# The down projection of a feed-forward layer as a 2x2 block product with seven products

## The chip, the core and the metric

One core of a Trainium2 chip runs the kernel. The metric is the time of one execution on the device in microseconds (us), the median of three runs. Four engines matter here: TensorE (PE in the rows, with its weight loads as PEld), VectorE (DVE), ScalarE (ACT) and GpSimd (POOL). SyncE (SP) issues nearly all transfers; its queue is SPq in the rows.

## What is computed

Two layers follow each other; the change touches the end of the second one, its feed-forward part:

```
h = rmsnorm(x, norm2_g)                                    # x: 512 tokens x 2048
x = x + (silu(h @ ffn_w_gate) * (h @ ffn_w_up)) @ ffn_w_down   # 2048 -> 5632 -> 2048
return rmsnorm(x, final_norm_g)
```

The down projection is the last product: 512 x 5632 by 5632 x 2048. All of it is float32. The kernel gets float32 precision out of TensorE by writing each operand as a high part h and a residual l in a rounded format (`split`, L136 and L122: ScalarE copies to h, VectorE subtracts h from the raw value to get l) and by adding up three products: high by high, high by residual, residual by high. So every block product costs three matmuls.

## The kernel before

Each matmul multiplies a 128x128 stationary tile by a 128x512 moving tile. A program-wide planner orders the instructions of each engine's queue by priority and by its own idea of durations, and puts in all waits; an engine's queue then runs strictly in that order. `high_priority(n)` moves the instructions under it n places ahead.

The feed-forward part runs in `finish` in two stages.

*Gate and up.* The 5632 hidden features are done in 11 groups of 512. `fast_group` treats gate and up weights of a group together, as a 2x2 block product in which eight block products are replaced by seven, each of a sum of operands by a sum of weights. Operand sums are made once (`fast_operands`, VectorE, then split). Weight sums are made for each group by VectorE (`chained`, L122, the rows fr<-fr,fr), in the raw tiles that the loads filled; the pool of raw tiles has 10 buffers of [128, 2, 512]. `part` then splits a half product's weights (two 128-row tiles, 512 columns) and issues 12 matmuls: eight that use the high weights (pp<-wh), four that use the residual (pp<-wl). I call such a set of 12 a unit. High and residual weights have three buffers each. A product is accumulated in a PSUM tile pp of two banks; there are three such tiles. The finished hidden features are transposed and stored to a scratch tensor in memory, ud.

*Down.* For this stage the raw pool is replaced by one with 3 buffers and PSUM is split anew into eight single banks, tiles psm. A running sum acc (facc in the rows, 512 tokens x 2048) is loaded with the residual stream x3d (L1780). The hidden features come back in 11 chunks of 512 (`hidden`, L1786, two chunks ahead) and are split. For chunks 0 to 9, `down` goes over four blocks of 512 output columns; for each, `block` loads and splits the weights (L146, 512 KB a load) and issues 4 feature tiles x 4 token tiles x 3 = 48 matmuls; VectorE adds the four banks onto acc. Chunk 10 keeps all its weights at hand (L1812) and goes token tile by token tile, so that each tile's final norm and store (L1835) can follow its last add.

All transfers above are issued by SP, in one queue. GpSimd does only small powers for the norms there.

Of the kernel before, what the change touches and what calls it, by code (L numbers as in the profile page):

```python
# [17 lines left out]
D = 2048  # L18
# [75 lines left out]
class Kernel:  # L94
# [1494 lines left out]
    def fast_operands(self, pool, za, zb, tiles):  # L1589
        ta, tb = slice(0, 256), slice(256, 512)  # L1590
        x5 = self.t(pool, [128, 4, 256], F32, "fx5")
        x6 = self.t(pool, [128, 4, 256], F32, "fx6")
        x7 = self.t(pool, [128, 4, 256], F32, "fx7")
# [4 lines left out]
        for i, x in ((1, za[:, :, ta]), (7, x7), (5, x5), (6, x6), (4, None), (3, zb[:, :, tb]), (2, zb[:, :, ta])):  # L1598
            if i == 4:
                x = x7  # L1600
                self.tt(x, zb[:, :, ta], x6, ALU.add)
            o = tiles()
            h, l = (o[:, k:k + 2, :].rearrange("p a (b t) -> p (a b) t", t=256) for k in (0, 2))
            self.split(h, l, x)
            out[i] = (h, l)
        return out


    def halves(self, raw, pools):
        pools.append(pools.pop(0))  # L1610
        h = self.t(pools[0], [128, 2, 512], F32R, "wh")
        l = self.t(pools[0], [128, 2, 512], F32R, "wl")
        self.split(h, l, raw)
        return h, l

    def fast_group(self, srcs, X, rp, cp, wps, parts):
        nc, tc = self.nc, self.tc
        W = {}  # L1620
# [18 lines left out]
        ps = {}  # L1639

        def part(i, u, opens):
            with tc.high_priority(self.ahead):
                h, l = self.halves(weight[i](u), wps)
            at = [(2 * u + kk, kk, t) for kk in range(2) for t in range(2)]

            for j, kk, t in at:
                xh, xl = (x[:, j % 4, t * 128:t * 128 + 128] for x in X[j // 4][i])
                self.mm(ps[i][:, t, :], xh, h[:, kk, :], opens and j == 0, False, not opens)
                self.mm(ps[i][:, t, :], xl, h[:, kk, :], False, False, not opens)
            for j, kk, t in at:  # L1650
                xh = X[j // 4][i][0][:, j % 4, t * 128:t * 128 + 128]
                self.mm(ps[i][:, t, :], xh, l[:, kk, :], False, j == 7, not opens)
# [7 lines left out]
        for p in parts:  # L1660
            for i in (1, 7, 5):
# [4 lines left out]
                if p[-1] == 3 and i == 1:  # L1666
                    p1 = result("p1")
# [28 lines left out]
    def finish(self):  # L1696
        tc, nc, a = self.tc, self.nc, self.a
        NC = 11
# [3 lines left out]
        with self.pool("ff0", 1) as f0:  # L1702
# [3 lines left out]
            with self.pool("opx", 2) as opx:  # L1706
                X = []
                made = [0]

# [4 lines left out]
                with self.pool("w21", 1) as p1, self.pool("w22", 2) as p2, self.pool("w23", 3) as p3:  # L1714
# [3 lines left out]
                    for n, b in enumerate((0, 2, 1, 3)):  # L1718
# [20 lines left out]
                        if n % 2 == 0:  # L1739
                            za = z  # L1740
                        else:
                            X.append(self.fast_operands(p1, za, z, tiles))
# [10 lines left out]
                with self.pool("fr", 10, side="right") as rp, self.pool("fc", 1) as cp, self.pool("fu", 2) as up, self.pool("fw", 1) as fw:  # L1753
# [20 lines left out]
            self.raw_pool = self.pool("wq", 3, side="right")  # L1774
            self.wp = self.raw_pool.__enter__()
            self.psum_pools(4, 4)
            with self.pool("ff1", 2) as p1, self.pool("ff2", 1) as p2:
                acc = self.t(p2, [128, 4, D], F32, "facc")
                for t in range(4):
                    nc.sync.dma_start(out=acc[:, t, :], in_=x3d[t])  # L1780
                fg = self.t(p2, [128, D], F32, "fg")
                nc.sync.dma_start(out=fg, in_=a["final_norm_g_2"].rearrange("(o d) -> o d", o=1).to_broadcast([128, D]))

                def hidden(c):
                    u = self.four(F32)
                    nc.sync.dma_start(out=u, in_=ud[c * 4:c * 4 + 4].rearrange("f p t -> p f t"))  # L1786
                    h4, l4 = self.four(F32R), self.four(F32R)
                    self.split(h4, l4, u)
                    return [(h4[:, j, :], l4[:, j, :]) for j in range(4)]

                def down(c, hs):
                    for b in range(4):
                        ps = [self.psm() for _ in range(4)]
                        self.block(wd[c * 512:c * 512 + 512], [(b * 512, 512)], 4,
                                   [(ps[t], "t", (t, 0), hs, True, True) for t in range(4)])
                        for t in range(4):
                            v = acc[:, t, b * 512:b * 512 + 512]
                            self.tt(v, v, ps[t], ALU.add)

                hs = [hidden(0), hidden(1)]  # L1800
                for c in range(NC - 1):
                    down(c, hs[c])
                    if c + 2 < NC:
                        hs.append(hidden(c + 2))

                c = NC - 1
                W = []
                for b in range(4):
                    h4, l4 = self.four(F32R), self.four(F32R)
                    for k in range(0, 4, 2):  # L1810
                        raw = self.t(self.wp, [128, 2, 512], F32, "raw")
                        nc.sync.dma_start(out=raw, in_=wd[c * 512 + k * 128:c * 512 + k * 128 + 256, b * 512:b * 512 + 512].rearrange("(k p) c -> p k c", p=128))  # L1812
                        self.split(h4[:, k:k + 2, :], l4[:, k:k + 2, :], raw)
                    W.append((h4, l4))
                for t in range(4):
                    s4 = self.t(p1, [128, 4], F32, "s4")
                    tk = slice(t * 128, t * 128 + 128)
                    for b in range(4):
                        ps = self.psm()
                        for k in range(4):  # L1820
                            xh, xl = hs[c][k]
                            self.mm(ps, xh[:, tk], W[b][0][:, k, :], k == 0, False)
                            self.mm(ps, xh[:, tk], W[b][1][:, k, :], False, False)
                            self.mm(ps, xl[:, tk], W[b][0][:, k, :], False, k == 3)
                        v = acc[:, t, b * 512:b * 512 + 512]
                        self.tt(v, v, ps, ALU.add)
                        j = self.t(p1, [128, 512], F32, "g")
                        self.act(j, v, AF.Square, accum_out=s4[:, b:b + 1])
# [3 lines left out]
                    for b in range(4):  # L1832
                        o = slice(b * 512, b * 512 + 512)
                        self.stt(acc[:, t, o], acc[:, t, o], r4, fg[:, o], ALU.mult, ALU.mult)
                        nc.sync.dma_start(out=self.out[0, tk, o], in_=acc[:, t, o])  # L1835
# [33 lines left out]
```

## Time and profile before

| | before |
|---|---|
| median of 3 runs | 3597.96 us (3597.35 to 3599.32) |
| time of the profiled execution | 3597.96 us |
| span of its trace, first to last instruction | 3596.1 us |
| PE busy | 3507.5 us (98%) |
| DVE busy | 2173.8 us (60%) |
| ACT busy | 1368.8 us (38%) |
| mean granted clock of TensorE | 0.985 of full speed |

The profile is of one execution. Busy time of PE is modelled from pipelined matmuls, so a busy PE need not be at its peak. Where the rows name a buffer, the number behind it is left out: wh and wl are high and residual weights, fr and raw are raw weight tiles, op are operand tiles, acc, pp and psm are PSUM tiles.

### The profile page before, as it was taken

The page shows a single profiled execution, that of the slowest core. Times are in us where ns is not written, and L with a number is a line of the kernel's source. Part 1 is how long each engine was busy: PE and PEld are TensorE (multiplying, and loading weights), DVE is VectorE, ACT ScalarE, POOL GpSimd, SP SyncE. Part 2 cuts the span into 40 slices and gives each one's busy share as a digit, 9 for nine tenths or more (in the row PEclk, how much of TensorE's full clock was granted, in tenths as well). Part 3 has the DMA queues.
Part 4 walks back from the last instruction along what each step waited for, and adds up shares of the span by engine and source line. Part 5 has one row for each costly group of instructions (what it writes and reads, how often), then busy time and mean ns, then how long its engine had stood idle before and what let it go on. Part 6 is the DMA issues. An engine that isn't in the chain of part 4 may idle for free.

```text
span 3596.1 us, 48583 instructions
## 1 busy us (share of the span) xinstructions
PE 3507.5 (98%) x18850; PEld 2748.8 (76%) x18850; DVE 2173.8 (60%) x3432; ACT 1368.8 (38%) x2225; POOL 55.7 (2%) x50
## 2 busy tenths in 40 slices
PE   6899999999999999999999998999999999999998
PEld 3486668777778788788877786888888888788887
DVE  3364555456554545675466557777788788555445
ACT  3333443356533323443233334444444444322212
POOL 0000000000000000000000000000000000000000
PEclk8999999999999999999999999999999999999999
DMA  8813333322144353334444443334443344534333
GB/s 278 283 36 112 99 100 88 95 67 82 48 138 147 107 149 109 112 116 116 132 121 129 145 141 129 117 117 127 131 122 107 118 123 141 187 122 126 99 100 106
DMA packets 352602, 442.22 MB, mean 123 GB/s; under 512 B 45871, under 2 KB 200179, under 8 KB 351731
## 3 DMA queue, kind: packets, MB, share of 16 engines
q1 hardware_dynamic: 349456, 437.82, 39.9%
q8 instruction: 148, 2.42, 0.3%
q10 hardware_dynamic: 2915, 1.29, 0.1%
q14 instruction: 83, 0.68, 0.1%
HBM read 383.45 MB, written 55.57 MB: 122 GB/s over the span
## 4 chain that ended last, share of the span: by engine, by line
PE 93%; DMA 3%; DVE 2%; ACT 1%; issue 0%; SPq 0%; POOL 0%; DVEq 0%; ACTq 0%; POOLq 0%
PE acc L112 44%; PE psm L112 23%; PE pp L112 23%; PE psm L116 2%; DMA wm<-in_w_mod_dram 1%; PE pt L116 1%; DVE wl L122 0%; DMA xr<-in_x_dram 0%; DMA raw<-in_ffn_w_down_dram 0%; DMA ym<-ysd 0%; DVE op L122 0%; PE acc L116 0%; DMA xr<-in_ctx_dram 0%; DMA fr<-in_ffn_w_up_dram 0%; DVE s L122 0%
## 5 line engine op out<-in xcount | busy, mean ns | idle before, releaser
L112 PE MATMUL acc<-op,wh 128*128 128x512 f32 (+2 forms) x4160 | 1254.5, 390 | 14.8 <-DVE sl L132 4.6
L112 PEld LDWEIGHTS acc<-op,wh 128*128 128x128 f32 (+1 forms) x4160 | 764.1, 189 | 229.5 <-issue 54.9
L122 DVE TENSOR_TENSOR wl<-raw,wh 128x512 fp32r<-128x512 f32 (+4 forms) x464 | 421.0, 908 | 690.0 <-ACT wh L136 641.1
L112 PE MATMUL acc<-op,wl 128*128 128x512 f32 (+2 forms) x2080 | 773.0, 389 | 2.1 <-DVE wl L122 2.1
L136 ACT CAST wh<-raw 128x512 fp32r<-128x512 f32 (+4 forms) x464 | 369.1, 796 | 1028.3 <-PE acc L112 637.7
L112 PE MATMUL pp<-wh,op 128*128 128x512 f32 x2112 | 529.9, 393 | 10.2 <-ACT wh L136 10.1
L136 ACT CAST wh<-fr 128x1024 fp32r<-128x1024 f32 x308 | 323.1, 1052 | 402.0 <-PE pp L112 350.2
L112 PEld LDWEIGHTS acc<-op,wl 128*128 128x128 f32 (+1 forms) x2080 | 390.4, 189 | 108.7 <-issue 26.9
L112 PEld LDWEIGHTS pp<-wh,op 128*128 128x128 f32 x2112 | 397.4, 188 | 99.3 <-ACT wh L136 10.7
L122 DVE TENSOR_TENSOR wl<-fr,wh 128x1024 fp32r<-128x1024 f32 x308 | 371.1, 1220 | 100.5 <-ACT wh L136 65.5
L112 PE MATMUL psm<-wh,op 128*128 128x512 f32 x1280 | 396.2, 391 | 7.3 <-DVE facc L122 7.3
L112 PEld LDWEIGHTS psm<-wh,op 128*128 128x128 f32 x1280 | 241.4, 189 | 58.2 <-issue 7.7
L112 PE MATMUL pp<-wl,op 128*128 128x512 f32 x1056 | 285.3, 392 | 0.2 <-DVE wl L122 0.2
L112 PE MATMUL psm<-wl,op 128*128 128x512 f32 x640 | 250.1, 391 | 0.3 <-DVE wl L122 0.3
L122 DVE TENSOR_TENSOR fr<-fr,fr 128x1024 f32<-128x1024 f32 x176 | 211.1, 1220 | 50.9 <-DMA fr<-in_ffn_w_gate_dram 33.0
L112 PEld LDWEIGHTS pp<-wl,op 128*128 128x128 f32 x1056 | 197.9, 188 | 43.6 <-DVE wl L122 0.6
L122 DVE TENSOR_TENSOR facc<-facc,psm 128x512 f32<-128x512 f32 x176 | 118.0, 686 | 60.6 <-PE psm L112 54.2
L112 PEld LDWEIGHTS psm<-wl,op 128*128 128x128 f32 x640 | 120.7, 189 | 25.7 <-DVE wl L122 0.7
L112 PE MATMUL acc<-wm,cs 128*32 128x512 f32 x384 | 126.1, 616 | 11.8 <-DMA wm<-in_w_mod_dram 11.8
L112 PE MATMUL acc<-wh,op 128*128 128x256 f32 x576 | 114.8, 293 | 0.0
L112 PEld LDWEIGHTS acc<-wh,op 128*128 128x128 f32 x576 | 91.9, 192 | 5.2 <-issue 3.8
L112 PE MATMUL pp<-wh,opx 128*128 128x512 f32 x352 | 93.8, 399 | 0.0
(469 smaller groups left out, 3506.0 us busy)
## 6 DMA issues: line engine op xcount, KB each, us to landing
raw<-in_w_in_dram SPq DMA_DIRECT2D x216, 256.0 KB, 2.8
fr<-in_ffn_w_gate_dram SPq DMA_DIRECT2D x88, 512.0 KB, 4.1
fr<-in_ffn_w_up_dram SPq DMA_DIRECT2D x88, 512.0 KB, 4.0
raw<-in_ffn_w_down_dram SPq DMA_DIRECT2D x88, 512.0 KB, 3.8
wm<-in_w_mod_dram SPq DMA_DIRECT2D x64, 512.0 KB, 5.8
raw<-in_w_out_dram SPq DMA_DIRECT2D x64, 512.0 KB, 3.8
raw<-in_w_in_dram SPq DMA_DIRECT2D x240, 128.0 KB, 2.4
wm<-in_w_mod_dram SPq DMA_DIRECT2D x64, 256.0 KB, 2.8
```

The lines of the kernel that those rows point to most:

```text
L112: self.nc.tensor.matmul(out, lhsT=l, rhs=r, start=start, stop=stop, skip_group_check=more)
L116: self.nc.tensor.transpose(out, x, self.ident[0:n, 0:n])
L122: (e or self.nc.vector).tensor_tensor(out=out, in0=x, in1=y, op=op)
L136: self.nc.scalar.copy(h, x)
```

## The change

Chunks 0 to 9 of the down stage become five chunks of eight feature tiles (1024 features), each done twice, for the left and the right 1024 output columns (`v`). One such pass is a 2x2 block product (two halves of features, two halves of columns; the 512 tokens are cut into two halves as well) done with seven products in place of eight, in the order 1, 7, 2, 5, 4, 6, 3. Chunk 10 stays as it was, except for its buffers.

Operand sums are made by `fast_operands`, as in the stage before; its temporaries now come from the raw pool. Weight sums are made by transfers: a load puts one block's weights into a raw tile, and a second transfer, issued by GpSimd (`nc.gpsimd.dma_start(..., accum_op=ALU.add)`), adds another block's weights onto them where they lie. Products 7, 6 and 3 reuse the raw tiles of product 1 in that way, each after the split of the product before it in that chain has read them; product 5 adds onto a tile of its own. PSUM and raw pool of the stage before are kept (three tiles of two banks, ten raw tiles), product 2 is accumulated in the bank of product 1, 4 in that of 7, 3 in that of 5. acc is no longer loaded first: in the first chunk the products are copied to it, and then GpSimd's accumulating transfers add x3d.

The twelve matmuls of a unit move into a helper `product`, which the stage before uses too.

```diff
-    def fast_operands(self, pool, za, zb, tiles):
+    def fast_operands(self, temps, za, zb, tiles, order=(1, 7, 5, 6, 4, 3, 2)):
...
-        x5 = self.t(pool, [128, 4, 256], F32, "fx5")
+        x5, x6, x7 = temps(), temps(), temps()
...
+    def product(self, X, i, ps, h, l, j0, opens, last):
+        at = [(j0 + kk, kk, t) for kk in range(2) for t in range(2)]
+
+        for j, kk, t in at:
+            xh, xl = (x[:, j % 4, t * 128:t * 128 + 128] for x in X[j // 4][i])
+            self.mm(ps[:, t, :], xh, h[:, kk, :], opens and j == 0, False, not opens)
+            self.mm(ps[:, t, :], xl, h[:, kk, :], False, False, not opens)
+        for j, kk, t in at:
+            xh = X[j // 4][i][0][:, j % 4, t * 128:t * 128 + 128]
+            self.mm(ps[:, t, :], xh, l[:, kk, :], False, j == last, not opens)
...
-            self.raw_pool = self.pool("wq", 3, side="right")
-            self.wp = self.raw_pool.__enter__()
-            self.psum_pools(4, 4)
             with self.pool("ff1", 2) as p1, self.pool("ff2", 1) as p2:
+                wps = [self.wp2, self.wp2, p2]
                 acc = self.t(p2, [128, 4, D], F32, "facc")
-                for t in range(4):
-                    nc.sync.dma_start(out=acc[:, t, :], in_=x3d[t])
...
+                au = [self.t(p2, [128, 2, 512], F32, f"au{v}") for v in range(2)]
...
+                order = (1, 7, 2, 5, 4, 6, 3)
+
+                def operands(c):
+                    with tc.high_priority(400):
+                        z = []
+                        for i in range(2):
+                            z.append(self.four(F32))
+                            f = (2 * c + i) * 4
+                            nc.sync.dma_start(out=z[i], in_=ud[f:f + 4].rearrange("f p t -> p f t"))
+                        return [self.fast_operands(lambda: raw().rearrange("p a (b t) -> p (a b) t", t=256), z[0], z[1],
+                                                   lambda: self.four(F32R), order)]
+
+                def down(c, v, X):
...
+                    def load(name, u):
+                        r = raw()
+                        nc.sync.dma_start(out=r, in_=source(name, u))
+                        if name == "a11":
+                            W[u] = r
+                        return r
...
+                    def plus(r, name, u):
+                        nc.gpsimd.dma_start(out=r, in_=source(name, u), accum_op=ALU.add)
+                        return r
+
+                    weight = {
+                        1: lambda u: load("a11", u), 7: lambda u: plus(W[u], "a21", u), 2: lambda u: load("a12", u),
+                        5: lambda u: plus(load("a21", u), "a22", u), 4: lambda u: load("a22", u),
+                        6: lambda u: plus(W[u], "a22", u), 3: lambda u: plus(W[u], "a12", u),
+                    }
...
+                    onto = {2: 1, 4: 7, 3: 5}
+                    to = {1: U, 7: A22, 2: A11, 5: A22, 4: A21, 6: U, 3: A12}
+                    for i in order:
+                        ps[i] = ps[onto[i]] if i in onto else bank()
+                        for u in range(2):
+                            with tc.high_priority(self.ahead):
+                                h, l = self.halves(weight[i](u), wps)
+                            self.product(X, i, ps[i], h, l, 2 * u, i not in onto, 3)
+                        if c == 0 and i not in (5, 6):
+                            nc.scalar.copy(to[i], ps[i])
+                        else:
+                            self.tt(to[i], to[i], ps[i], ALU.subtract if i == 5 else ALU.add)
+                    if c == 0:
+                        for t in range(4):
+                            o = slice(v * 1024, v * 1024 + 1024)
+                            nc.gpsimd.dma_start(out=acc[:, t, o], in_=x3d[t][:, o], accum_op=ALU.add)
+                    if c == NC // 2 - 1:
+                        self.tt(A21, A21, U, ALU.subtract)
+                        self.tt(A22, A22, U, ALU.subtract)
+                        self.tt(A12, A12, U, ALU.add)
+
+                X = operands(0)
+                for c in range(NC // 2):
+                    down(c, 0, X)
+                    down(c, 1, X)
+                    if c + 1 < NC // 2:
+                        X = operands(c + 1)
...
                 c = NC - 1
+                with tc.high_priority(400):
...
```

## Rows read from the trace of the kernel before

**Rows 1.** Page, part one: busy time, share and instructions of each engine.

```profile
PE 3507.5 (98%) x18850; PEld 2748.8 (76%) x18850; DVE 2173.8 (60%) x3432; ACT 1368.8 (38%) x2225; POOL 55.7 (2%) x50
```

**Rows 2.** Page, part four: the chain that ended last, by engine.

```profile
PE 93%; DMA 3%; DVE 2%; ACT 1%; issue 0%; SPq 0%; POOL 0%; DVEq 0%; ACTq 0%; POOLq 0%
```

**Rows 3.** Chain in order of time: start, duration (us), what.

```profile
2378.80 16.73 PE pp L112 x73
2396.41 59.48 PE pp L112 x259
...
2457.70 16.79 PE pp L112 x73
...
3125.24 391.31 PE psm L112 x1725
```

**Rows 4.** Waits of TensorE from 2200 us on: total, times, longest.

```profile
PE psm L112 <- DVE facc L122: 10.8, 2, 7.3
```

**Rows 5.** Stretches: PE, PEld, DVE, ACT, POOL, clock, DMA share, GB/s.

```profile
2400.00:2800.00 400.00, 400.00 (x1785) 327.70 (x1784) 319.70 (x293) 180.49 (x193) 0.00 (x0) 1.00 0.40 121
3160.00:3500.00 340.00, 340.00 (x1501) 281.53 (x1501) 169.32 (x191) 72.62 (x66) 0.00 (x0) 1.00 0.36 110
```

**Rows 6.** SP's queue in order of time: two loads of hidden features.

```profile
3190.16 0.37 SPq L1786 DMA_DIRECT2D op<-ud  x1
...
3233.68 0.37 SPq L1786 DMA_DIRECT2D op<-ud  x1
```

**Rows 7.** Groups of instructions from 2200 us on: busy, mean ns, idle before.

```profile
L122 DVE TENSOR_TENSOR fr<-fr,fr 128x1024 f32<-128x1024 f32 x176 | 211.1, 1220 | 50.9 <-DMA fr<-in_ffn_w_gate_dram 33.0
...
L122 DVE TENSOR_TENSOR wl<-raw,wh 128x1024 fp32r<-128x1024 f32 x80 | 97.9, 1224 | 173.2 <-ACT wh L136 172.9
...
L122 DVE TENSOR_TENSOR c<-pp,un 128x1024 f32<-128x1024 f32 x11 | 13.4, 1217 | 0.0
```

**Rows 8.** Timeline in gate/up: start, duration, what, idle before.

```profile
2263.09 1.08 PE L112 MATMUL pp<-wl,op 128*128 128x512 f32 x4
2263.29 1.05 ACT L136 CAST wh<-fr 128x1024 fp32r<-128x1024 f32 x1 [1.72 <-PE pp L112]
2264.01 1.98 PE L112 MATMUL pp<-wh,op 128*128 128x512 f32 x8
2264.37 1.23 DVE L122 TENSOR_TENSOR wl<-fr,wh 128x1024 fp32r<-128x1024 f32 x1 [1.54 <-ACT wh L136]
```

**Rows 9.** DMA issues: KB each, median us from issue to landing.

```profile
fr<-in_ffn_w_up_dram SPq DMA_DIRECT2D x88, 512.0 KB, 4.0
...
wm<-in_w_mod_dram SPq DMA_DIRECT2D x64, 512.0 KB, 5.8
...
op<-ud SPq DMA_DIRECT2D x11, 1024.0 KB, 5.5
```

**Rows 10.** GpSimd (POOL) in order of time: a tiny operation after a long wait.

```profile
2214.45 1.87 POOL L122 TENSOR_TENSOR r3s<-r3s,mhalf 128x4 f32<-128x4 f32 x1 [188.68 <-DVE r3s L129]
...
3556.69 0.55 POOL L122 TENSOR_TENSOR r<-r,mhalf 128x1 f32<-128x1 f32 x1 [1340.37 <-DVE r L129]
```

**Rows 11.** Stretches: loads of w_mod at the start, a burst of weight loads later.

```profile
40.00:80.00 40.00, 30.01 (x129) 10.45 (x129) 12.23 (x32) 9.57 (x18) 0.28 (x1) 0.91 0.88 290
...
2221.00:2223.00 2.00, 2.00 (x6) 1.52 (x6) 1.80 (x2) 0.97 (x1) 0.00 (x0) 0.50 1.05 389
```

**Rows 12.** TensorE in order of time, handover from gate/up to down.

```profile
3110.63 0.77 PE L112 MATMUL psm<-wh,op 128*128 128x512 f32 x1 [7.32 <-DVE facc L122]
...
3116.06 0.40 PE L112 MATMUL psm<-wl,op 128*128 128x512 f32 x1
```

**Rows 13.** TensorE in order of time, start of the last chunk.

```profile
3541.75 45.44 PE L112 MATMUL psm<-op,op 128*128 128x512 f32 x192 [3.46 <-DVE facc L122]
```

**Rows 14.** Stretches behind that start.

```profile
3543.00:3544.00 1.00, 1.00 (x4) 0.71 (x4) 1.00 (x3) 0.33 (x1) 0.00 (x0) 0.50 0.87 317
...
3545.00:3546.00 1.00, 1.00 (x5) 0.76 (x4) 0.78 (x2) 0.95 (x1) 0.00 (x0) 0.59 0.00 0
```

More of the change, by code (lines that the diff above doesn't have):

```diff
@@ L1597, in fast_operands @@
         out = {}
[L1598 removed]
+        xs = {1: za[:, :, ta], 7: x7, 5: x5, 6: x6, 4: x7, 3: zb[:, :, tb], 2: zb[:, :, ta]}
+        for i in order:
+            x = xs[i]
             if i == 4:
[L1600 removed]
                 self.tt(x, zb[:, :, ta], x6, ALU.add)
@@ L1643, in part @@
                 h, l = self.halves(weight[i](u), wps)
[L1644 to L1652, printed above, removed]
+            self.product(X, i, ps[i], h, l, 2 * u, opens, 7)
         def bank():
@@ L1708, in finish @@
                 made = [0]
+                fx = iter(range(100))
                 def tiles():
@@ L1741, in finish @@
                         else:
-                            X.append(self.fast_operands(p1, za, z, tiles))
+                            X.append(self.fast_operands(lambda: self.t(p1, [128, 4, 256], F32, f"fx{next(fx) % 3}"), za, z, tiles))
                     r = self.token_rsq(f0, s3, D, 1e-6, "r3s")
@@ new lines, in raw, with bank @@
+                def raw():
+                    return self.t(rp, [128, 2, 512], F32, "fr")
+                def bank():
+                    return self.t(self.pp, [128, 2, 512], F32, "pp")
+                order = (1, 7, 2, 5, 4, 6, 3)
[8 more added lines that the diff above has]
+                                                   lambda: self.four(F32R), order)]
@@ new lines, in down, with source @@
+                def down(c, v, X):
+                    n1 = slice(v * 1024, v * 1024 + 512)
+                    n2 = slice(v * 1024 + 512, v * 1024 + 1024)
+                    W = {}
+                    ps = {}
+                    def source(name, u):
+                        k = (c * 8 + (4 if name[2] == "2" else 0) + 2 * u) * 128
+                        return wd[k:k + 256, n1 if name[1] == "1" else n2].rearrange("(k p) c -> p k c", p=128)
+                    def load(name, u):
[12 more added lines that the diff above has]
+                    }
+                    A11, A12, A21, A22, U = acc[:, 0:2, n1], acc[:, 2:4, n1], acc[:, 0:2, n2], acc[:, 2:4, n2], au[v]
+                    onto = {2: 1, 4: 7, 3: 5}
+                    to = {1: U, 7: A22, 2: A11, 5: A22, 4: A21, 6: U, 3: A12}
+                    for i in order:
+                        ps[i] = ps[onto[i]] if i in onto else bank()
[15 more added lines that the diff above has]
+                        self.tt(A12, A12, U, ALU.add)
@@ L1788, in hidden @@
-                    self.split(h4, l4, u)
-                    return [(h4[:, j, :], l4[:, j, :]) for j in range(4)]
-                def down(c, hs):
+                    uh, ul = self.four(F32R), self.four(F32R)
+                    self.split(uh, ul, u)
+                    W = []
                     for b in range(4):
[L1793 to L1814, printed above, removed]
+                        h4, l4 = self.four(F32R), self.four(F32R)
@@ new lines, in finish @@
+                        for k in range(0, 4, 2):
+                            r = raw()
+                            nc.sync.dma_start(out=r, in_=wd[c * 512 + k * 128:c * 512 + k * 128 + 256, b * 512:b * 512 + 512].rearrange("(k p) c -> p k c", p=128))
+                            self.split(h4[:, k:k + 2, :], l4[:, k:k + 2, :], r)
+                        W.append((h4, l4))
+                    fg = []
+                    for i in range(2):
+                        fg.append(raw())
+                        nc.sync.dma_start(out=fg[i].rearrange("p a b -> p (a b)"),
+                                          in_=a["final_norm_g_2"][i * 1024:i * 1024 + 1024].rearrange("(o d) -> o d", o=1).to_broadcast([128, 1024]))
```

27 lines of the change are left out of this document (12 added, 15 removed).

## The prediction, made before the changed kernel was run

> **What bounds the kernel now.** I read the page's shares first: TensorE is busy for 3507.5 of 3596.1 us, VectorE 60%, ScalarE 38% [rows 1]. The chain that ended last lies on TensorE for 93% [rows 2]. Then the chain in order of time: the down stage is one unbroken piece, 1725 matmuls in 391.31 us, 0.2268 us each [rows 3]. Waits of TensorE from 2200 us on: for the down stage only the two waits for facc, 10.8 us in all [rows 4]. And stretches: from 3160 to 3500 us TensorE is busy throughout at full granted clock (2.4 GHz), while VectorE works half of the time and the transfers move 110 GB/s [rows 5]. So the stage is matmul issue and nothing else: a chunk of 192 matmuls takes 43.52 us, from one load of hidden features to the next [rows 6]. Only fewer matmuls, or the waits at its two ends, can shorten it, and whatever feeds the matmuls has room.
>
> **Fewer matmuls.** Ten chunks of 192 are 1920; now five chunks x two passes x seven products x 24 are 1680. Their form is that of the stage before (stationary operand sums, moving weight halves), which runs 259 in 59.48 us, 0.2297 us each, 1% slower [rows 3]. 1920 x 0.2268 = 435.5; 1680 x 0.2297 = 385.9. Gain 49.6 us, if nothing waits. A unit of 12 then takes 2.75 us, a pass of 14 units 38.6 us, a chunk 77.2 us.
>
> **The two ends.** Before, the down stage began with a wait of 7.32 us for acc's load [rows 12]. The next 13 matmuls took 5.43 us where 13 x 0.2268 = 2.95 would do, so 9.8 us went there. That load is gone: the first products are copied. What may be late next is that first copy, whose target lies in memory that the last group's buffers held; I give back 2.3 (0 to 5). Gain 7.5. The last chunk began with 3.46 us idle [rows 13], behind which the granted clock was at its lower level until about 3545.5 [rows 14], some 1.5 us more. The wait was for an add on VectorE, behind splits that waited for raw weights through 3 buffers; there are ten now. Gain 4 of these 5 (0 to 5).
>
> **Work beside the matmuls.** VectorE, per chunk: 28 residuals, 14 adds of products, 11 operations for operand sums, all of 1024 elements a partition at 1.22 us [rows 7]: 53 x 1.22 = 64.7 of 77.2 us, 84%. The stage before runs at 319.7 of 400, 80%, and TensorE doesn't wait [rows 5]. I count nothing for it on average, but an operation that is needed at once now finds VectorE taken. ScalarE, some 40 us of 77, is covered. So are the added operand loads: same bytes, issued far ahead. PSUM: a bank has at least one product (5.5 us) between its last matmul and its next, for an add of 1.22 [rows 7].
>
> **The accumulating transfers.** No row shows one, nor any transfer of GpSimd's. Eight per pass, 80 in all, each 512 KB, and 8 more for x3d in the first chunk. Each reads its destination as well as its source. What matters is the time from the residual that frees a raw tile to the landed sum, D. Of the chain 1, 7, 6, 3 the steps 1 to 7 and 6 to 3 are neighbours in the order, so two units apart: 2 tight steps a pass, 20 in all. (7 to 6 has eight units between, 5's load and addition run ahead.)
>
> How long may D be? In the stage before, a unit's high part starts at 2263.29, released by the last high matmul of the unit three before it; its residual is done at 2264.37 + 1.23 = 2265.60; the unit after the running one starts at 2264.01 [rows 8], so its own matmuls start at 2264.01 + 2 x 2.75 = 2269.5 and those of the unit two later at 2275.0. That one's high part, 1.05 us, must start by 2273.9. So D up to 2273.9 - 2265.6 = 8.3 us costs nothing; each us beyond is idle time of TensorE, 20 times, as the buffers allow no further running ahead.
>
> How long is it? Below: a plain 512 KB load lands in 4.0 us. The nearest row for twice the reading is the 1 MB load, 5.5 us [rows 9]. Under load, 512 KB took 5.8 in place of 4.0 [rows 9], at 290 GB/s [rows 11]. Here a chunk moves 10.5 MB plainly (16 weight loads, 2 MB of features) and 8.4 MB by addition: 18.9 MB in 77.2 us are 245 GB/s, and 354 if the added bytes count twice; bursts of such loads reached 389 [rows 11]. So I take 5.5 x 5.8 / 4.0 = 8.0, and 0.6 for GpSimd to start, as its smallest operation takes (0.55 to 1.87, [rows 10]). Half of a 1.22 us operation ahead on VectorE comes out of the allowance: 8.0 + 0.6 + 0.6 - 8.3 = 0.9 too long, say 0.8. Cost 20 x 0.8 = 16 us. Ends: 4.0 + 0.6, which costs 0, and twice 5.8 + 1.9 = 13.5, which with VectorE's 0.6 costs 5.8 a step, 116 in all.
>
> *A rule that weighs on this.* The Trainium skill ("Collectives: The Full Stack", The bandwidth ceiling: the fold count and why AG ≠ RS ≠ AR) says that an add in a transfer costs no cycles of its own but needs two source reads on one ring, and so halves the rate. No row here shows it. By it the demand would be the 354 GB/s above, under the 389 of the burst: busy transfers and late sums, but no bound.
>
> Behind a waiting addition on GpSimd's queue stand only the additions that follow, and x3d's four: if the planner put these ahead of pass two's first sum, that would be late once, by some 5 us. Who waits for it is ScalarE's and then VectorE's split, in order, and behind these the adds that free banks. On SP's queue the ten raw tiles turn over once in little more than a pass: the operand sums' three temporaries push the next chunk's first weights back to a tile that the last split of the pass frees. Loaded in 4.0, split in 2.3, they come about 1 us late: 4 chunk changes, 4 us (0 to 12).
>
> **Sum** against the profiled execution: 3596.1 - 49.6 - 7.5 - 4 + 16 + 4 = 3555.0. It lasted 3597.96, the median itself, 1.9 beyond its span. So **3557 us**.
>
> **Rivals.**
> *Fully hidden.* D stays below 8.3, as the plain row and the fact that a burst runs at 389 speak for: only chunk changes cost, 3541; with better ends 3537. Against it: VectorE at 84%, 245 GB/s at least.
> *GpSimd and VectorE get in each other's way.* GpSimd's start comes late by up to one VectorE operation, 1.2 us, at each tight step: 20 x 1.2 = 24 more, 3581. For it: VectorE has hardly a gap in which GpSimd would be alone. Against: GpSimd's only rows are single operations after long waits [rows 10] and show neither. The Trainium skill ("SBUF — State Buffer", Who interferes with whom) has GpSimd and VectorE share a pair of ports, through which GpSimd's transfers write their descriptors; by it copies lock them out, while two-input adds, which most of these are, should not. No row here shows that.
> *Late sums, slower than before.* The price per tight step grows with D. Without the 16 the forecast is 3541, 57 below the median of before; 57 / 20 = 2.85, so from D = 8.3 + 2.85 - 0.6 = 10.5 on the change loses. At 12.5, between that and the upper end of 13.5, a step waits 4.8; a wait of 3.46 also cost 1.5 of lower clock [rows 13, 14]: 20 x 6.3 = 126, 3667. For it: two additions of a product follow each other, and the second may queue behind the first. Against: the 1 MB row.
> *The transfers bound the stage, slower.* If an added byte takes three times a plain one, a chunk asks for 10.5 + 3 x 8.4 = 35.7 MB; at 389 GB/s that is 91.8 us, 14.6 over 77.2, 73 in five chunks on 3541: 3614. It decides from 2.85 times on: then a chunk takes 57 / 5 = 11.4 longer. For it: transfers now work at 0.36 share for 110 GB/s [rows 5], so 0.80 for 245 already at one time. Against: the burst.
> *No gain that shows*: the late sums near 2.85, 3598.
> That the seven products don't come to 1680 matmuls I see no way for.
>
> **How the numbers follow.** Forecast (waits of 0 to 2 us at the tight steps) 0.42, its own range 3541 to 3581; fully hidden 0.20; VectorE in the way 0.10; no gain 0.04; late sums 0.13; bound by transfers 0.11. What a measurement can tell from no change is 0.2%, 7 us. Faster 0.72, same 0.04, slower 0.24. The range is 3533 to 3618: it holds all but most of the late sums and a few hundredths below.
>
> **What would show it.** 1680 matmuls of the down form at 0.23 us, in the stretches. Waits of TensorE for ScalarE's high parts, at products 7 and 3 alone, some 20, below 2 us each: right. None: hidden. Waits at every product, and the transfers' share near 1: bound. Waits above 3 us with the granted clock falling behind each: late sums. GpSimd's issue rows beside VectorE's decide the ports. The handover should show at most 5 us idle. The prediction is wrong if the chain in the down stage leaves TensorE for GpSimd's transfers for more than 60 us, or if TensorE waits at steps other than these.

## The result, and the profile after

The changed kernel takes 3647.7 us (median; 3646.7 to 3651.3), against 3597.7 for the kernel before in the same comparison: 1.014 of it, interval 1.012 to 1.016. It is slower by 50 us where I had forecast 41 us faster, and it lies outside my range.

Busy time on the page of the changed kernel, for [rows 1]:

```profile
PE 3488.6 (96%) x18610; PEld 2718.1 (75%) x18610; DVE 2252.7 (62%) x3443; ACT 1453.5 (40%) x2320; POOL 159.6 (4%) x138
```

The 240 matmuls are gone (18850 to 18610), but TensorE's busy time fell by only 19 us. Waits of TensorE from 2900 us on (total, times, longest), for [rows 4]; pt belongs to the end of the stage before, au takes the first copy of product 1:

```profile
PE pp L112 <- ACT wh L136: 76.1, 23, 9.6
PE pt L116 <- DVE s L132: 3.3, 2, 2.7
PE pp L112 <- ACT au L1841: 1.1, 1, 1.1
PE pp L112 <- DVE wl L122: 0.7, 1, 0.7
```

The chain that ended last, by engine, for [rows 2]:

```profile
PE 31%; DMA 5%; issue 4%; DVE 2%; POOL 1%; ACT 1%; POOLq 0%; DVEq 0%; ACTq 0%; SPq 0%
```

This chain could be followed back to 2049 us only, so its shares add up to 44% of the span. The stage that had waited twice, for facc, now waits 23 times for high parts (wh, which ScalarE makes). ScalarE isn't slow: what released its casts was a transfer (rows further down). Stretches of the down stage (columns as in [rows 5]):

```profile
3150.00:3250.00 100.00, 81.24 (x320) 63.79 (x319) 51.49 (x45) 39.03 (x39) 23.53 (x21) 0.91 0.96 220
3250.00:3350.00 100.00, 83.99 (x345) 67.36 (x345) 62.04 (x54) 36.17 (x37) 19.32 (x16) 0.93 0.82 189
3350.00:3450.00 100.00, 83.16 (x332) 65.64 (x331) 63.03 (x56) 36.60 (x36) 19.35 (x16) 0.91 0.81 189
3450.00:3550.00 100.00, 89.27 (x363) 70.76 (x361) 67.03 (x58) 36.71 (x35) 21.73 (x18) 0.95 0.85 196
```

VectorE works at 51 to 67%, not at the 84% forecast, while the transfer engines work at a share of 0.81 to 0.96 for only 189 to 220 GB/s. The queues on the page (packets, MB, share of 16 engines over the span) say why:

```profile
q1 hardware_dynamic: 349024, 433.63, 38.7%
q0 software_dynamic: 22912, 46.14, 7.4%
```

Plain bytes: 433.63 MB in 0.387 x 3645.8 = 1411 us, 307 GB/s at full share. GpSimd's queue q0, all of it additions: 46.14 MB in 270 us, 171 GB/s. An added byte holds the engines 1.8 times as long. The 307 is a mean over the whole kernel with all its other loads; in the down stage alone (3088 to 3593 us, shares of these 505 us) it is more:

```profile
q0 software_dynamic: 22912, 46.14, 53.4%
q1 hardware_dynamic: 27108, 51.90, 30.5%
```

There plain bytes moved at 337 GB/s of full share and the additions at 171 again, so within the stage the ratio is 2.0. Landing times (KB each, median us), for [rows 9]:

```profile
fr<-in_ffn_w_down_dram SPq DMA_DIRECT2D x88, 512.0 KB, 6.4
fr<-in_ffn_w_down_dram POOLq DMA_DIRECT2D x80, 512.0 KB, 8.9
```

Now one stall in order of time. TensorE at products 7 and 3 of successive passes:

```profile
3260.74 3.34 PE L112 MATMUL pp<-wh,op 128*128 128x512 f32 x8 [3.41 <-ACT wh L136]
3299.75 6.67 PE L112 MATMUL pp<-wh,op 128*128 128x512 f32 x16 [9.62 <-ACT wh L136]
3306.26 1.09 PE L112 MATMUL pp<-wl,op 128*128 128x512 f32 x4
3307.18 2.02 PE L112 MATMUL pp<-wh,op 128*128 128x512 f32 x8
```

ScalarE just ahead of the first two:

```profile
3259.64 1.99 ACT L136 CAST wh<-fr 128x1024 fp32r<-128x1024 f32 x2 [6.74 <-DMA fr<-in_ffn_w_down_dram]
...
3298.65 1.99 ACT L136 CAST wh<-fr 128x1024 fp32r<-128x1024 f32 x2 [11.11 <-DMA fr<-in_ffn_w_down_dram]
```

GpSimd's additions (1.20 us each to issue):

```profile
3253.62 1.23 POOL L1823 DMA_DIRECT2D fr<-in_ffn_w_down_dram  x1 [16.90 <-DVE wl L122]
...
3279.62 1.20 POOL L1823 DMA_DIRECT2D fr<-in_ffn_w_down_dram  x1 [12.77 <-ACT wh L136]
3281.40 1.20 POOL L1823 DMA_DIRECT2D fr<-in_ffn_w_down_dram  x1 [0.58 <-DMA fr<-in_ffn_w_down_dram]
3282.99 2.44 POOL L1823 DMA_DIRECT2D fr<-in_ffn_w_down_dram  x2 [0.39 <-DVE wl L122]
```

and SP's queue at that time:

```profile
3279.14 0.92 SPq L1800 DMA_DIRECT2D op<-ud  x2
3280.45 0.37 SPq L1816 DMA_DIRECT2D fr<-in_ffn_w_down_dram  x1
```

Product 7's addition is issued at 3253.62 and read at 3259.64: 6.0 us. Product 3's is issued at 3282.99 and read at 3298.65: 15.7 us. Ahead of it on GpSimd's queue went both additions of the next pass's product 5 (3279.62 and 3281.40), just ahead on SP's the next chunk's 2 MB of hidden features. After the wait, eight matmuls take 3.3 to 3.8 us, where they take 2.0 otherwise.

### The profile page after: what moved, and what is told of

It reads as the page before. It is cut to its first block, busy times and chain, and to the rows that moved or that the text cites. A ratio compares the mean times of both kernels' runs of the same rounds, so it can differ in the third digit from the quotient of the medians.

```text
span 3645.8 us, 48490 instructions
## 1 busy us (share of the span) xinstructions
PE 3488.6 (96%) x18610; PEld 2718.1 (75%) x18610; DVE 2252.7 (62%) x3443; ACT 1453.5 (40%) x2320; POOL 159.6 (4%) x138
## 3 DMA queue, kind: packets, MB, share of 16 engines
q1 hardware_dynamic: 349024, 433.63, 38.7%
q0 software_dynamic: 22912, 46.14, 7.4%
## 5 line engine op out<-in xcount | busy, mean ns | idle before, releaser
L112 PE MATMUL pp<-wh,op 128*128 128x512 f32 x3232 | 833.8, 402 | 87.4 <-ACT wh L136 86.0
L112 PEld LDWEIGHTS pp<-wh,op 128*128 128x128 f32 x3232 | 621.2, 193 | 237.7 <-ACT wh L136 97.0
L136 ACT CAST wh<-fr 128x1024 fp32r<-128x1024 f32 x448 | 468.2, 1051 | 674.7 <-PE pp L112 453.8
L122 DVE TENSOR_TENSOR wl<-fr,wh 128x1024 fp32r<-128x1024 f32 x448 | 539.8, 1220 | 263.5 <-ACT wh L136 209.1
L122 DVE TENSOR_TENSOR wl<-raw,wh 128x512 fp32r<-128x512 f32 (+4 forms) x384 | 322.9, 841 | 519.5 <-ACT wh L136 482.9
L136 ACT CAST wh<-raw 128x512 fp32r<-128x512 f32 (+4 forms) x384 | 284.9, 743 | 721.0 <-PE acc L112 611.6
L112 PE MATMUL pp<-wl,op 128*128 128x512 f32 x1616 | 438.7, 395 | 0.7 <-DVE wl L122 0.7
L112 PEld LDWEIGHTS pp<-wl,op 128*128 128x128 f32 x1616 | 307.1, 191 | 69.5 <-DVE wl L122 1.2
L122 DVE TENSOR_TENSOR fr<-fr,fr 128x1024 f32<-128x1024 f32 x176 | 211.0, 1220 | 47.5 <-DMA fr<-in_ffn_w_gate_dram 32.5
L1823 POOL DMA_DIRECT2D fr<-in_ffn_w_down_dram x80 | 98.2, 1282 | 1255.4 <-DMA fr<-in_ffn_w_down_dram 968.1
L112 PE MATMUL acc<-wl,op 128*128 128x256 f32 x288 | 85.3, 297 | 0.0
```

Source lines behind the costliest of these rows:

```text
L112: self.nc.tensor.matmul(out, lhsT=l, rhs=r, start=start, stop=stop, skip_group_check=more)
L122: (e or self.nc.vector).tensor_tensor(out=out, in0=x, in1=y, op=op)
L136: self.nc.scalar.copy(h, x)
L1823: nc.gpsimd.dma_start(out=r, in_=source(name, u), accum_op=ALU.add)
```

## The experiments

Two theories. *Engine time*: by the figures above a chunk's transfers want 10.5 MB / 307 + 8.4 MB / 171 = 34.2 + 49.1 = 83.3 us, and TensorE wants 77.2; the stage asks for more than there is. (As a bound and nothing else that would cost 5 x 6.1 = 31 us; with the stage's own 337 GB/s the chunk comes to 80.3, and it would cost 15.) *Late landings at tight steps*: the additions of 7 and 3 come too late for their places in the order, whatever the engines' total. (Behind each time stands its ratio to the kernel before, with the interval.)

**No weight sums.** The addition is dropped; products take the plain tiles.

```diff
-                        nc.gpsimd.dma_start(out=r, in_=source(name, u), accum_op=ALU.add)
```

> The changed kernel without the 80 accumulating transfers of weights (products 7, 5, 6 and 3 use unsummed weights; the eight for x3d stay). If these transfers cause the loss, TensorE's 23 waits for high parts in the down stage (some 80 us, most followed by a few us at the lower clock) go, and the time is 3535 to 3550 us, the prediction's 3541 without waits. If VectorE at 84%, the banks or the matmuls' form cost the time, it stays above 3590.

3532.7 us, 0.982 [0.980, 0.984], 2 us below the guess. Its stretch 3150 to 3500, and TensorE's waits for high parts:

```profile
3150.00:3500.00 350.00, 349.76 (x1525) 285.57 (x1524) 268.66 (x237) 158.79 (x163) 4.09 (x5) 1.00 0.43 135
```

```profile
PE pp L112 <- ACT wh L136: 2.4, 3, 1.9
```

This is the floor: 0.2294 us a matmul, no wait worth naming. So matmuls, ends, VectorE and banks are innocent, and all 115 us hang on the 80 additions.

**Plain transfers in their place.** They overwrite the tile; queue, size, waits as changed.

```diff
-  nc.gpsimd.dma_start(out=r, in_=source(name, u), accum_op=ALU.add)
+  nc.gpsimd.dma_start(out=r, in_=source(name, u))
```

> The same 80 transfers from the same queue at the same places behind the same waits, but plain: they overwrite the raw tile instead of adding to it (the sums are left out). Theory 1, an accumulating transfer reads twice and so holds the shared transfer engines about twice as long: the median landing falls from 8.9 us to about 6, waits in the down stage fall below 25 us in all, 3550 to 3575 us. Theory 2, what is late is GpSimd's queue (1.2 us to issue, the next pass's product 5 ahead of product 3, in order): landing changes little, 3615 us or more.

3581.3 us, 0.996 [0.995, 0.998]. The queue and its landing:

```profile
q0 software_dynamic: 12672, 46.14, 4.2%
...
fr<-in_ffn_w_down_dram POOLq DMA_DIRECT2D x80, 512.0 KB, 5.6
```

The same bytes hold the engines for 4.2% of 3579.4 = 150 us and not 270, and 66 of the 115 us come back: adding has a price of its own. The landing is as theory 1 had it, the time lies between the two guesses. The other 49 us are there without any addition of weights, and not for want of engine time: 18.9 MB a chunk at 307 GB/s are 61.6 of 77.2 us.

**Additions of an eighth of the size.**

```diff
-  nc.gpsimd.dma_start(out=r, in_=source(name, u), accum_op=ALU.add)
+  nc.gpsimd.dma_start(out=r[:, :, 0:64], in_=source(name, u)[:, :, 0:64], accum_op=ALU.add)
```

> The 80 accumulating transfers at their places in the order, waited for as changed, but each adds only the first 64 of 512 columns (64 of 512 KB): an eighth of the bytes (the sums are incomplete). Share of the transfers near that without sums, 0.45 to 0.55. If an addition comes late because of the engine time of its bytes, landing falls to 3 to 5 us and the time to 3535 to 3555. If it comes late because of the place in the order alone (tile free, issue, queue), landings stay at 6 and more and the time above 3580.

3561.4 us, 0.990 [0.989, 0.992], 6 us above the guess. Queue, landing, and TensorE's waits for high parts:

```profile
q0 software_dynamic: 22912, 9.44, 2.3%
...
fr<-in_ffn_w_down_dram POOLq DMA_DIRECT2D x80, 64.0 KB, 3.7
```

```profile
PE pp L112 <- ACT wh L136: 14.9, 7, 4.4
```

With waits, issues and order as changed, 86 of 115 us are gone. The packets are the same 22912, and they took 2.3% of the span, 82 us in place of 270: bytes are most of the cost. 29 us stay, seven waits (14.9 us in all) and the clock behind them.

**Product 3's additions first on GpSimd's queue**, the next pass's product 5 behind them.

```diff
+  with tc.issue_after(self.third) if name == "a22" and r is not W[u] and self.third else ExitStack():
+      ins = nc.gpsimd.dma_start(out=r, in_=source(name, u), accum_op=ALU.add)
+  if name == "a12":
+      self.third = ins.ins
```

> Only GpSimd's queue is put in another order: the two additions of the next pass's product 5 come behind those of product 3 instead of ahead of them. Theory 2: the longest waits, all at product 3 (3 to 10 us), shrink to 0 to 3 us each, and the time falls by 35 to 55 us, to 3590 to 3615. Theory 1: the transfers still share the engines with the loads of the next pass, so product 3 gains only the 1 to 3 us that it stood behind the others, and the time stays above 3625.

3615.4 us, 1.005 [1.003, 1.007]: 32 us back with not a byte less. Landings fall to 7.9 us; TensorE's waits:

```profile
PE pp L112 <- ACT wh L136: 52.7, 18, 6.8
```

Order counts, and isn't all.

**A wide order**: 1, 5, 2, 7, 6, 4, 3 in two chains, with four units or more between a split and the next use of its tile.

```diff
-  order = (1, 7, 2, 5, 4, 6, 3)
+  order = (1, 5, 2, 7, 6, 4, 3)
...
+  1: lambda u: load("a11", u), 5: lambda u: plus(load("a21", u), "a22", u), 2: lambda u: load("a12", u),
+  7: lambda u: plus(W["a11", u], "a21", u), 6: lambda u: plus(W["a21", u], "a11", u),
+  4: lambda u: load("a22", u), 3: lambda u: plus(W["a21", u], "a12", u),
...
```

> All eight sums by accumulating transfers as changed, but products in the order 1, 5, 2, 7, 6, 4, 3, with one addition chain a11 to 7 and the other a21 to 5 to 6 to 3, so that an addition has four units (11 us) or more between the split that frees its tile and its own unit. Bytes and engine time as changed: 17.1 for loads + 24.6 for additions = 41.7 us in a pass of 38.6. Theory late landings alone: 3535 to 3550, waits gone. Theory engine time alone: ten passes x 3.1 above the floor of 3532.7, so 3560 to 3575, share near 1. Both, with landings of 9 to 16 us as in the changed kernel: some waits stay, 3575 to 3610. If the order counts for nothing: 3630 to 3650.

3614.8 us, 1.005 [1.004, 1.007], just above the guess for both. Each step is twice as wide or more; what TensorE waits for now comes mostly once a chunk (timeline of TensorE, then of GpSimd and ScalarE, then the stretch between, and one period from stall to stall):

```profile
3187.08 3.78 PE L112 MATMUL pp<-wh,op 128*128 128x512 f32 x8 [10.46 <-ACT wh L136]
...
3282.32 0.80 PE L112 MATMUL pp<-wh,op 128*128 128x512 f32 x1 [10.66 <-ACT wh L136]
3371.08 0.80 PE L112 MATMUL pp<-wh,op 128*128 128x512 f32 x1 [9.46 <-ACT wh L136]
```

```profile
3261.34 1.20 POOL L1822 DMA_DIRECT2D fr<-in_ffn_w_down_dram  x1 [12.32 <-DVE op L122]
3262.70 3.68 POOL L1822 DMA_DIRECT2D fr<-in_ffn_w_down_dram  x3 [0.15 <-DMA fr<-in_ffn_w_down_dram]
```

```profile
3281.22 1.05 ACT L136 CAST wh<-fr 128x1024 fp32r<-128x1024 f32 x1 [16.72 <-DMA fr<-in_ffn_w_down_dram]
```

```profile
3261.00:3281.00 20.00, 10.66 (x47) 8.38 (x45) 6.93 (x7) 1.79 (x2) 4.88 (x4) 0.88 1.05 270
3282.32:3371.08 88.76, 79.30 (x337) 64.33 (x337) 61.66 (x54) 35.57 (x36) 19.35 (x16) 0.94 0.88 209
```

Four additions go out together beside the next loads, two of the next chunk's product 5 and then two of product 3; with the engines full (1.05) product 3's first sum is read 18 us after its issue. Counted off from the stage's start (24 matmuls a product), the long stalls, these three and a fourth of 9.0 us at 3460.84, all stand at product 3 of a chunk's second pass. They are 95 and 89 us apart, where a chunk of matmuls is 77.2 and the transfers want 83.3 or less, and over the period shown the engines' share is 0.88 only. So the sum is late in the crowd at the chunk's end; that the engines' total sets the pace is not shown.

**Additions aside, first try.** Half of them went into a tile of their own, half onto a11's second tile.

```diff
+  nc.gpsimd.dma_start(out=W["a11", 1] if u else aside, in_=source(name, u), accum_op=ALU.add)
```

> The 80 accumulating transfers stay, with their size and queue, but add into tiles that no product reads; the products take plain loads (so no weight sums). Nothing waits for an addition; the transfers' engine time is as changed (41.7 us for a pass of 38.6, worked out from the shares). Theory engine time: loads come late, 3560 to 3600, transfers' share above 0.9, waits of TensorE behind loads. Theory late landings, where the engines' time is no bound of its own: 3533 to 3548, as without the transfers. Rival, GpSimd's descriptor writing slows VectorE: its 1220 ns an operation would grow.

3650.1 us, 1.015 [1.014, 1.017], and not to be read as a price: two stalls of 39 us each come from loads that waited for a tile which an addition still held (SP's queue waited 237 us for such). One stretch of such a stall measures additions nearly by themselves:

```profile
3285.00:3300.00 15.00, 0.00 (x0) 0.00 (x0) 0.00 (x0) 0.00 (x0) 3.75 (x4) 0.50 1.04 184
```

Full share at 184 GB/s.

**Additions aside, in a tile of their own.**

```diff
+  for k in range(2 - u):
+      nc.gpsimd.dma_start(out=aside[:, :, u * 352:u * 352 + 352], in_=source(name, u)[:, :, k * 160:k * 160 + 352], accum_op=ALU.add)
```

> As the version with the additions aside, but they go into a tile of their own, so that no load waits for one of them: for each pair of units three transfers of 352 of 512 columns (in all 46 MB again, 120 transfers). Products take plain loads, no weight sums. All that is left of the additions is their engine time: 24.6 us for them + 17.1 for plain loads in a pass of 38.6. Theory engine time: a chunk cannot go below 83.4 us where TensorE wants 77.2, so 3563 or more, up to 3600 with the granted clock falling behind waits, share above 0.9. Theory that only their places in the order cost: 3533 to 3548.

3691.9 us, 1.026 [1.024, 1.028], above both guesses, and the most telling run. Its stretches in the stage and behind it:

```profile
3150.00:3440.00 290.00, 282.96 (x1222) 230.18 (x1221) 216.09 (x185) 131.44 (x128) 89.76 (x76) 0.99 1.01 232
3525.00:3645.00 120.00, 0.00 (x0) 0.00 (x0) 0.00 (x0) 0.00 (x0) 26.47 (x22) 0.50 0.47 64
```

TensorE, with full transfer engines (1.01), keeps its pace: the plain loads it needs still come in time (8.7 us, median). What falls behind is the additions. Of this size (352 KB) 70 were issued in those 290 us, 25.2 MB, where twelve for each 38.6 us would be 32.5: 78%. (Only two can be under way, one into each half of the tile, but the engines were full all the same.) The rest ran behind the stage, 5.4 us apart, and the tiny power for the first token tile's norm stood behind them on GpSimd's queue (VectorE's timeline):

```profile
3649.05 2.74 DVE L132 SCALAR_TENSOR_TENSOR facc<-facc,r,fr 128x512 f32<-128x512 f32 x4 [143.04 <-POOL r L122]
```

TensorE's one wait of 140.1 us there is most of the loss: 3691.9 - 140.1 = 3552 would be left. So full engines slow the loads (8.7 us, 4.4 in the floor run), but these are issued early enough; it is additions that come too late, and TensorE pays only where a product waits for one. Both theories hold a part: order alone gave back 32 and 33 us, with every byte as it was, and less engine time alone (plain transfers, small additions) 66 and 86, with the order as it was. I read them as one mechanism, in which engine time gives the size and the order the places; that reading is argued.

**Sums by GpSimd's own additions.**

```diff
+  def plus(to, name, u, e=nc.gpsimd):
+      r = W[to, u]
+      self.tt(r, r, W.get((name, u)) if (name, u) in W else load(name, u), ALU.add, e)
...
```

> Weight sums as additions computed by GpSimd from the eight raw tiles of a pass, in the order of the stage before; no accumulating transfer of weights, 8 plain loads a pass. GpSimd's 512-element addition took 1.04 us, so 2.1 us for 1024, 8 a pass: 17 of 38.6 us. Theory 1: the transfers fall back to about 110 to 140 GB/s, no wait at products 7 and 3, 3540 to 3560 us. If GpSimd and VectorE get in each other's way on the memory that both read, VectorE's two-input operations lengthen beyond 1.22 us, and at 84% busy it then becomes the bound: 3580 to 3640.

3608.2 us, 1.003 [1.002, 1.005]. VectorE's residuals and GpSimd's additions (groups, 3150 to 3500; one fence for each engine):

```profile
L122 DVE TENSOR_TENSOR wl<-fr,wh 128x1024 fp32r<-128x1024 f32 x109 | 213.6, 1985 | 18.3 <-ACT wh L136 12.8 <-PE pp L112 5.2
```

```profile
L122 POOL TENSOR_TENSOR fr<-fr,fr 128x1024 f32<-128x1024 f32 x62 | 191.4, 3132 | 158.6 <-DVE wl L122 119.8 <-DMA fr<-in_ffn_w_down_dram 26.0 <-issue 12.8
```

The residuals take 1985 ns beside them and 1220 elsewhere: compute on GpSimd does get in VectorE's way. The Trainium skill ("SBUF — State Buffer", SBUF: two separate sides) says that a two-input VectorE operation and a GpSimd operation that reads this memory hold their shared ports one at a time; the row agrees.

**Sums by VectorE: all, or two of four.** All, in the order as changed (where no engine is named, `tt` runs on VectorE):

```diff
+  def plus(to, name, u, e=None):
+      r = W[to, u]
+      self.tt(r, r, W.get((name, u)) if (name, u) in W else load(name, u), ALU.add, e)
...
+  1: lambda u: load("a11", u), 7: lambda u: plus("a11", "a21", u), 2: lambda u: load("a12", u),
+  5: lambda u: plus("a21", "a22", u), 4: lambda u: W["a22", u],
+  6: lambda u: plus("a11", "a22", u), 3: lambda u: plus("a11", "a12", u),
```

> All eight weight sums of a pass by VectorE, in the raw tiles, as in the stage before; no accumulating weight transfer. Floor without any sums: 3532.7, with VectorE busy for 268.7 of 350 us there. Eight additions of 1.22 us are 9.8 us of a pass of 38.6, 89 us of 350, so VectorE would be at 357 of 350: it becomes the bound by 2%. Both theories on the transfers (engine time, and late landings): 3540 to 3580, waits of TensorE for ScalarE's or VectorE's weights at many steps, share of the transfers about 0.4. If GpSimd's transfers were not what costs, it would not fall below 3615.

3552.8 us, 0.989 [0.987, 0.991]. Its stretch:

```profile
3150.00:3500.00 350.00, 337.62 (x1444) 270.20 (x1443) 334.56 (x293) 155.61 (x154) 3.52 (x4) 1.00 0.43 136
```

VectorE is at 334.56 of 350 us, 96%, and TensorE waits 14 us in all.

Only the two tight steps, 7 and 3, on VectorE (`add`, with the same body as `plus` just above; `plus` is the accumulating transfer again):

```diff
+  1: lambda u: load("a11", u), 7: lambda u: add("a11", "a21", u), 2: lambda u: load("a12", u),
+  5: lambda u: plus(W["a21", u], "a22", u), 4: lambda u: load("a22", u),
+  6: lambda u: plus(W["a11", u], "a22", u), 3: lambda u: add("a11", "a12", u),
```

> Order as changed; the sums of products 7 and 3 (the two tight steps) by VectorE, those of 5 and 6 by accumulating transfers. VectorE 268.7 + 9.07 passes x 4 x 1.22 = 313 of 350 (89%). Engine time of the transfers in a pass: loads 8 x 1.71 and 1 MB of hidden features 3.4, four additions x 3.07, together 29.4 of 38.6 us (share 0.76 at full pace). Theory engine time (an addition holds the engines 1.8 times as long and the stage wants more than it has): room again, 3535 to 3555. Theory late landings at the tight steps: the same, 3535 to 3555, since both are gone. Rival, additions come late at any step or GpSimd's issues get in VectorE's way: above 3575, with waits at 5 and 6.

3556.5 us, 0.989 [0.988, 0.991], just above the guess: 91 us back. GpSimd's additions land in 7.4 us, six waits for high parts remain (11.7 us). In the wide order, 6 and 3 on VectorE:

```diff
+  1: lambda u: load("a11", u), 5: lambda u: plus(load("a21", u), "a22", u), 2: lambda u: load("a12", u),
+  7: lambda u: plus(W["a11", u], "a21", u), 6: lambda u: add("a11", "a22", u),
+  4: lambda u: W["a22", u], 3: lambda u: add("a11", "a12", u),
```

> The wide order 1, 5, 2, 7, 6, 4, 3 with the sums of 5 and 7 by accumulating transfers and those of 6 and 3 by VectorE: share about 0.76 as in the version with two sums on VectorE in the order as changed, VectorE 89%. If room on the engines is what counts, both come out alike, 3535 to 3555. If the distance of the steps counts as well, this one is ahead by 5 to 20 us. If VectorE at 89% is the bound, both have waits for the residual weights and lie at 3550 to 3575.

3551.5 us (3544.6 to 3553.2), 0.987 [0.986, 0.989]. Its stretch:

```profile
3150.00:3500.00 350.00, 348.52 (x1515) 283.36 (x1514) 309.03 (x269) 161.68 (x161) 42.22 (x36) 1.00 0.72 188
```

Once the engines have room (0.72), the order is worth 5 us or nothing; the ranges of these two versions hardly differ by more than their runs do.

**One of four on VectorE, wide order**, for a demand just below what the engines have (the edit against the wide version):

```diff
-  4: lambda u: load("a22", u), 3: lambda u: plus(W["a21", u], "a12", u),
+  4: lambda u: load("a22", u), 3: lambda u: add("a21", "a12", u),
```

> Wide order, with the sum of product 3 alone on VectorE and those of 5, 7 and 6 by transfers: six additions x 3.07 + 17.1 = 35.5 us of engine time in a pass of 38.6 (0.92). Between the version with two sums on VectorE (29.4, 3544 to 3553) and that with none (41.7, 3614.8). Theory engine time as a bound: below it, so nearly all comes back, 3545 to 3565. Theory that each addition costs alike: half way, 3575 to 3590.

3558.0 us, 0.989 [0.987, 0.991]. The first sum taken off the transfers gives 57 us back, the second 6.5, so there is no one price for each addition. It looks like a bound crossed between 83.3 and 71 us of engine time in a chunk of 77.2. But the sum taken off is product 3's, the one at which the wide version's long stalls stood (39.6 of its 58.6 us of such waits). So this run can't tell the engines' total from the one late step; taking off the sum of 7 alone might, and was not run.

**The best of them, the first product 5 too on VectorE**, in the wide version with two sums:

```diff
+  return add("a21", "a22", u) if (c, v) == (0, 0) else plus(r, "a22", u)
```

> The version in the wide order with sums of 6 and 3 on VectorE and of 5 and 7 by transfers (3551.5, its profiled execution 3544.6), but in the very first pass product 5's sum by VectorE too, which takes away its wait of 6.3 us at 3108 and some 1.8 us at the lower clock behind it. 3535 to 3546. If VectorE, at the end of gate and up, is as late as the transfer: no gain, 3544 to 3553.

3545.3 us (3543.9 to 3546.2), 0.986 [0.985, 0.988]. Both kernels are beaten, the changed one by 102 us. The long wait at the stage's start is down from 6.3 us to 2.7 and 1.9; against the version before, whose runs reach 3544.6, no gain is shown.

## Why the prediction was wrong

**Right.** 240 fewer matmuls at 0.2294 us (I had 0.2297). The ends, in part: the wait for facc is gone, the first copies cost 1.1 us (I gave back 2.3), the last chunk begins without idle time; but the stage's first wait for a high part, 6.7 us (1.9 in the floor run), is more than the 5 that I had allowed for the handover. VectorE, forecast at 84%, was at 77% in the floor run and no bound. Chunk changes, forecast at 4 us, show no wait over 0.2 us in the floor run. The floor of 3532.7 lies a little below my "fully hidden". GpSimd's issuing didn't slow VectorE (1220 ns throughout). The places, too: counted off, 21 of the 23 waits for high parts, 67.6 of 76.1 us, stand at products 7 and 3.

**Wrong: the price of the tight steps.** I took D = 8.0 + 0.6 us for each of the 20 and 0.8 us of loss a step, 16 in all. The additions cost 115 us, 5.7 a step. It failed in three ways.

*Demand against capacity.* I set 245 to 354 GB/s against a burst of 389 [rows 11] and found room. The burst was 2 us long. My own other row, 110 GB/s at a share of 0.36 [rows 5], means 306 at full share, and 307 is what plain bytes got over the whole kernel. With it, and 1.8 for an added byte, the chunk is 83.3 us, and additions queue. The rival "transfers bound the stage" saw the full engines, but not how they cost; its threshold of 2.85 came from the burst. With 307 it falls to 88.6 x 307 / 1000 = 27.2 MB, less 10.5, over 8.4: 1.99 for a loss; the bound itself begins at 77.2 x 0.307 = 23.7 MB, so 1.57. The measured 1.8 lies between: as a bound alone it would have cost at most 31 of the 115 us, and the change would still have gained. (With the stage's own 337 the two come to 2.3 and 1.85, the ratio to 2.0: between again.) The rule quoted in the prediction from the Trainium skill ("Collectives: The Full Stack", The bandwidth ceiling: the fold count and why AG ≠ RS ≠ AR), an add halves the rate, is stated there for rings of collectives; these local transfers agree with it: 171 to 307 is 0.56, to the stage's 337 0.51.

*One D for twenty steps.* The median, 8.9 us, was nearly my 8.0 + 0.6. But seven of ten first additions of product 7 landed in 5.9 to 6.3 us. Product 3's first took 8.4 to 10.5 in a chunk's first pass and 13.1 to 15.6 in its second; in the last pass of all, with no next pass behind it, 6.0. I had listed what stands behind an addition on GpSimd's queue, and counted nothing for what is put ahead of it: the next pass's product 5, which runs ahead by right of priority, and, in a chunk's second pass, the 2 MB of features that I had called covered.

*Independent steps at 0.8 us, and the clock in the rival alone.* After a long stall at 3 the next splits come just in time, so that product 7's addition costs idle time at 6.0 us, below my allowance of 8.3. And matmuls at the lower clock stood behind most waits. Against the floor, the span is 114.3 us longer (3645.8 to 3531.5): 73.7 are waits for high parts (76.1 - 2.4). Most of the remaining 40.6 are matmuls at the lower clock: with the same 18610 matmuls TensorE's busy time is 34.7 us more (3488.6, and 3453.9 in the floor run), at a granted clock of 0.91 to 0.95 in the stretches, 1.00 in the floor.

A condition that I had named for being wrong is met: the chain has 4.9% of the span, 179 us, in transfers of down weights, 122 of them GpSimd's additions. The rival "late sums" came nearest, 3667 at 6.3 us a step, and in its mechanism as well: waits with the clock falling behind them.

Not settled: why the plain transfers in the additions' place still cost 49 us and the small ones 29. Their waits stand at the same steps (counted off, 25.4 of 27.4 us and 14.7 of 14.9 at products 7 and 3), but no run takes them apart further. Nor does a run show whether the engines' total costs anything beyond the late steps.

## What to carry to other kernels

Before work is moved to transfers, add up engine time for one period of the stage: plain bytes by the rate at full share that a long stretch shows (GB/s over share, not a burst), and an accumulated byte at 1.8 to 2 times that. If the sum comes near the period of the engine that bounds, expect late landings, and move a part elsewhere. Then, even where there is room, ask of each transfer that is needed soon what is queued ahead of it and beside it: a median landing says little about the one step that waits. Here two of the four sums on an engine with room brought the time that I had forecast, 3557, and a little better.

## Not expected of the hardware

- An accumulating transfer ran at 171 GB/s of full share, a plain one at 307 over the kernel and 337 in the stage.
- With saturated engines, SP's plain loads still came in 8.7 us, and GpSimd's additions fell to 78% of what was asked.
- GpSimd takes 1.20 us to issue one addition of 256 rows; a plain transfer of the same tile takes 0.72 (medians), one from SP 0.37.
- A GpSimd addition of 128x1024 took 3.13 us beside VectorE, whose residuals went from 1.22 to 1.99.
